# Latent attention: which engine sums the left-over column of the packed values

## The chip, the cores and the metric

The kernel runs on one core of a Trainium2 chip. The metric is the device time of one execution in microseconds (us); lower is better. The engines are called by their names in the profile: PE is TensorE's matmuls, PEld its weight loads, ACT is ScalarE, DVE is VectorE, POOL is GpSimd, SP is SyncE, which here only issues transfers.

## What is computed

The program is one encoder layer over 2048 tokens of width 1024: a Fourier mixing branch, a latent attention with 8 heads, an output projection, a cross attention to 256 memory tokens, and a mixture of 16 experts. The change lies in the latent attention:

```
s = einsum("bqhd,bkhd->bhqk", qn_b, k_nope) + einsum("bqhd,bkd->bhqk", qr_b, k_rope)
p = softmax(s * (64 + 32) ** -0.5)           # over all 2048 keys
o = einsum("bhqk,bkhd->bqhd", p, v)          # 64 channels of v for each head
```

All of it is wanted in float32 precision. The kernel multiplies in a rounded format (fp32r), so it splits operands into a high and a low part and adds the products high by high, high by low and low by high.

## The kernel before

**Work of the attention.** `phase_mla` goes over 32 units, each a head and a block of 512 queries, in an order written out by hand. A unit has 16 key tiles of 128 keys. For a key tile, `scores` makes three matmuls into a PSUM tile `pst` (lines 889 to 891; three such tiles are in turn), then ACT takes the exponential twice: rounded, into the SBUF tile `ph` (line 894), and exact, in place (line 895). DVE subtracts one from the other and gets the low part `pl` (line 909). The values follow three tiles later: `values` multiplies `ph` and `pl` by the value tile and adds into the unit's PSUM tile `po` (line 926).

**The left-over column.** A value tile `va` has 129 columns for each of its 128 keys: 64 columns of the high part, a column of ones that sums the exponentials, 63 columns of the low part, and as column 128 the low part of channel 0, for which the 128 columns of a weight load have no room. Its product with `ph` has to be added to row 0 of `po`. There are two ways. A tile in `BY_PE` gets another matmul with this one column as weights (line 928). For another tile, `ph` is multiplied by the column, a scalar for each partition, and added into an SBUF tile `acc`: POOL multiplies the tiles in `BY_POOL` (line 904), ACT the rest (line 906), both into one of two tiles `part`, and POOL adds (line 908). The first such tile of a unit writes `acc` itself. `whole` then sums `acc` over the partitions with a matmul by ones into row 0 (line 932), in slot 4 of the next unit, and ACT and DVE take the unit's result out of PSUM (lines 935 to 937).

**The order around it.** The loop over slots issues, for each key tile: the scores with their exponentials and the product for the left-over column, a step for the unit after (below), the subtraction, and the values of three tiles before; in 92 of 100 slots a step of the Fourier branch follows, which runs in the background (`bg`) on all engines. The step for the unit after finds the maximum of its scores for each query: 16 matmuls into one of two PSUM tiles `pmax` (line 837), each with a reduction on DVE (line 838). In slot 14 four transposes (line 846) and a copy by ACT (line 847) put the negative maxima into row 96 of the next unit's queries `q`. The third scores matmul of the next unit (line 891) reads that row, so it can't begin before the copy. Each engine executes its own instructions in the order of issue.

Of the kernel before, what the change touches and what calls it, by code (L numbers as in the profile page):

```python
# [10 lines left out]
F = mybir.dt.float32  # L11
R = mybir.dt.float32r
# [3 lines left out]
AF = mybir.ActivationFunctionType  # L16
OP = mybir.AluOpType
# [3 lines left out]
S, D, P = 2048, 1024, 128  # L21
# [9 lines left out]
def pool(ctx, tc, name, bufs=1, **kw):  # L31
    return ctx.enter_context(tc.tile_pool(name=name, bufs=bufs, reuse_waits="tile", **kw))
# [819 lines left out]
def phase_mla(e, keep):  # L852

    nc, tc = e.nc, e.tc
    scale = (ND + RD) ** -0.5
    with ExitStack() as ctx:
# [4 lines left out]
        pp = pool(ctx, tc, "mp", 3, side="right")  # L861
        mp = pool(ctx, tc, "mm", 2, side="right")
# [21 lines left out]
        def scores(h, c, kt):  # L884
            (kh, kl), q = KT[h], QT[h, c]
            qh, ql = q[:, 0], q[0:96, 1]
            p = ps.tile([P, 512], F, name="pst", bufs=3)
            ks = slice(kt * P, (kt + 1) * P)
            nc.tensor.matmul(p, kl[:, ks], qh[0:96], start=True, stop=False)  # L889
            nc.tensor.matmul(p, kh[0:96, ks], ql, start=False, stop=False)  # L890
            nc.tensor.matmul(p, kh[:, ks], qh, start=False, stop=True)  # L891
            ph = pp.tile([P, 512], R, name="ph", bufs=5)
            pl = pp.tile([P, 512], R, name="pl", bufs=3)
            nc.scalar.activation(ph, p, AF.Exp, scale=scale)  # L894
            nc.scalar.activation(p, p, AF.Exp, scale=scale)  # L895

            if kt not in BY_PE:
                w = VT[h, kt // 8][:, kt % 8, 128:129].bitcast(F)
                first = (h, c) not in AC
                if first:  # L900
                    AC[h, c] = mp.tile([P, 512], R, name="acc", bufs=1)
                t = AC[h, c] if first else mp.tile([P, 512], F, name="part", bufs=2)
                if kt in BY_POOL:
                    nc.gpsimd.tensor_scalar(t, ph.bitcast(F), w, None, op0=OP.mult)  # L904
                else:
                    nc.scalar.activation(t, ph.bitcast(F), AF.Copy, scale=w)  # L906
                if not first:
                    nc.gpsimd.tensor_add(AC[h, c], AC[h, c].bitcast(F), t)  # L908
            return ph, pl, lambda: nc.vector.tensor_sub(pl, p, ph.bitcast(F))  # L909

        OT, AC = {}, {}


        BY_PE, BY_POOL = (0, 1, 2, 3, 8, 15), (5, 7, 10, 12)

        rest = mp.tile([64, 1], F, name="rest", bufs=1)
        nc.gpsimd.memset(rest, 1.0)
# [2 lines left out]
        def values(h, c, kt, pr):  # L920

            if kt == 0:
                OT[h, c] = ps.tile([P, 512], F, name="po", bufs=2)
            v = VT[h, kt // 8][:, kt % 8]
            for i, t in enumerate(pr[:2]):
                nc.tensor.matmul(OT[h, c], v[:, 0:128], t, start=kt == 0 and i == 0, stop=False, skip_group_check=True)  # L926
            if kt in BY_PE:
                nc.tensor.matmul(OT[h, c][0:1], v[:, 128:129], pr[0], start=False, stop=False, skip_group_check=True)

        def whole(h, c):  # L930
# [34 lines left out]
        for n, (h, c) in enumerate(units):  # L965
            if n + 3 < len(units):
                load_q(n + 3)
            for kt in range(16):
                if kt in (1, 9) and c == 0 and h + 1 < H:
                    load_k(h + 1, kt // 8)  # L970
                if (c, kt) in ((1, 1), (3, 13)) and h + 1 < H:
                    load_v(h + 1, 4 * c - 4, 4 * c + 4)
                if n and kt == 4:
                    whole(*units[n - 1])
                pend.append((h, c, kt, scores(h, c, kt)))
                for m, i in ahead.get(slot, ()):
                    if i == 0:
                        MX[m] = max_steps(e, QT[units[m]], KT[units[m][0]][0], mp,
                                          lambda shape: ps.tile(shape, F, name="pmax", bufs=2))
                    MX[m][i]()  # L980
                pend[-1][3][2]()
                if len(pend) > 3:
                    values(*pend.pop(0))
                slot += 1
                if slot * RATE // 100 > (slot - 1) * RATE // 100:
                    next(bg, None)
                if (h and c == 0 or n == len(units) - 1) and kt in (4, 8, 12):
                    if kt == 4:
                        rs = recip(e, mp, nc.sync, h - 1) if c == 0 else recip(e, mp, nc.sync, h, 0, 1536)
                    next(rs)  # L990
        for u in pend:
            values(*u)
# [911 lines left out]
def run(e):  # L1904
    e.va_s = e.tc.dram_tile([H, P, 16 * VW], F, name="va_s")
    with ExitStack() as ctx:
        consts(e, ctx)
        pl = pool(ctx, e.tc, "aff")
        e.aff = pl.tile([P, 16, 16], F, name="aff")
        keep = ctx.enter_context(ExitStack())  # L1910
        phase_qkv(e)
        phase_mla(e, keep)
        cross = phase_cross(e)
        phase_out(e, keep, cross)
        for _ in cross:
            pass
        phase_moe(e)
# [141 lines left out]
```

## Time and profile before

| | |
|---|---|
| median of 3 runs | 3174.2 us (3169.05 to 3181.74) |
| the profiled execution's own time | 3177.02 us |
| span of its profile | 3175.2 us |
| mean granted clock of TensorE over the span | 0.972 |
| PE, PEld busy over the span | 2993.6 us (94%), 2583.3 us (81%) |
| DVE, ACT, POOL busy over the span | 1989.3 us (63%), 1669.6 us (53%), 1049.2 us (33%) |

The span is the stretch from the first to the last instruction; some 2 us of the execution lie around it. The attention takes the stretch from 280 to 1298 us. Busy times are unions over an engine's instructions. A matmul's end is modelled, so that the times of matmuls that follow each other overlap: the time that a matmul takes of PE is the distance of its start to the next one's start.

### The profile page before, as it was taken

The page shows a single profiled execution, that of the slowest core. Times are in us where ns is not written, and L with a number is a line of the kernel's source. Part 1 is how long each engine was busy: PE and PEld are TensorE (multiplying, and loading weights), DVE is VectorE, ACT ScalarE, POOL GpSimd, SP SyncE. Part 2 cuts the span into 40 slices and gives each one's busy share as a digit, 9 for nine tenths or more (in the row PEclk, how much of TensorE's full clock was granted, in tenths as well). Part 3 has the DMA queues.
Part 4 walks back from the last instruction along what each step waited for, and adds up shares of the span by engine and source line. Part 5 has one row for each costly group of instructions (what it writes and reads, how often), then busy time and mean ns, then how long its engine had stood idle before and what let it go on. Part 6 is the DMA issues. An engine that isn't in the chain of part 4 may idle for free.

```text
span 3175.2 us, 46609 instructions
## 1 busy us (share of the span) xinstructions
PE 2993.6 (94%) x17759; PEld 2583.3 (81%) x17759; DVE 1989.3 (63%) x3529; ACT 1669.6 (53%) x2715; POOL 1049.2 (33%) x1001
## 2 busy tenths in 40 slices
PE   7998989898999999899999998499999999999998
PEld 6997767677777676689888886499999999999998
DVE  5557877687878787565544445755555555555765
ACT  4445897687778787314433332244444444444554
POOL 1224668768765656200100001200001110002554
PEclk9999999899999999999999999699999999999999
DMA  6666152131121211375211112466666767667885
GB/s 197 208 211 184 41 168 65 28 76 51 44 65 49 68 36 50 100 202 187 90 60 60 61 54 76 135 205 207 199 214 211 216 211 224 204 201 235 298 306 204
DMA packets 314514, 452.51 MB, mean 143 GB/s; under 512 B 21185, under 2 KB 230337, under 8 KB 312946
## 3 DMA queue, kind: packets, MB, share of 16 engines
q1 hardware_dynamic: 282792, 373.08, 36.8%
q0 software_dynamic: 15216, 55.39, 5.7%
q10 hardware_dynamic: 16282, 21.06, 2.3%
q8 instruction: 140, 2.29, 0.3%
q14 instruction: 84, 0.69, 0.1%
HBM read 361.06 MB, written 88.28 MB: 142 GB/s over the span
## 4 chain that ended last, share of the span: by engine, by line
PE 56%; DVE 3%; POOL 1%; ACT 1%; issue 1%; DMA 0%; ACTq 0%; POOLq 0%; DVEq 0%
PE pa L45 5%; PE pa L46 5%; PE pa L47 5%; PE pb L46 5%; PE pb L45 5%; PE pb L47 5%; PE co L45 2%; PE co L47 2%; PE co L46 2%; PE sc L45 2%; PE sc L47 2%; PE sc L46 2%; PE py L45 2%; PE py L47 2%; PE py L46 2%; PE tr L1254 1%
## 5 line engine op out<-in xcount | busy, mean ns | idle before, releaser
L1702 DVE TENSOR_TENSOR wl<-wr,wh 128x2048 fp32r<-128x2048 f32 x188 | 429.6, 2292 | 265.0 <-ACT wh L1701 265.0
L1701 ACT ACTIVATE wh<-wr 128x2048 fp32r<-128x2048 f32 x191 | 362.9, 1908 | 128.9 <-issue 51.5
L909 DVE TENSOR_TENSOR pl<-pst,ph 128x512 fp32r<-128x512 f32 x512 | 351.3, 686 | 120.0 <-ACT pst L895 110.6
L908 POOL TENSOR_TENSOR acc<-acc,part 128x512 fp32r<-128x512 f32 x288 | 376.0, 1306 | 32.1 <-ACT part L906 11.3
L838 DVE TENSOR_REDUCE mt<-pmax 128x1 f32<-128x512 f32 x496 | 338.3, 683 | 68.1 <-PE pmax L837 66.1
L894 ACT ACTIVATE ph<-pst 128x512 fp32r<-128x512 f32 x512 | 304.9, 595 | 135.8 <-PE pst L891 130.5
L895 ACT ACTIVATE pst<-pst 128x512 f32<-128x512 f32 x512 | 305.2, 596 | 0.0
L1737 POOL DMA_INDIRECT x_s<-y,idx x24 | 63.5, 2648 | 730.9 <-ACT y L1872 637.5
L904 POOL TENSOR_SCALAR part<-ph,va 128x512 f32<-128x512 f32 x128 | 205.5, 1606 | 282.4 <-ACT ph L894 158.4
L45 PE MATMUL pa<-hh,wh 128*128 128x256 f32 x1024 | 293.1, 286 | 0.0
L46 PE MATMUL pa<-hl,wh 128*128 128x256 f32 x1024 | 290.7, 284 | 0.1
L47 PE MATMUL pa<-hh,wl 128*128 128x256 f32 x1024 | 290.5, 284 | 0.0
L45 PE MATMUL pb<-hh,wh 128*128 128x256 f32 x1024 | 289.8, 283 | 0.0
L46 PE MATMUL pb<-hl,wh 128*128 128x256 f32 x1024 | 289.8, 283 | 0.0
L47 PE MATMUL pb<-hh,wl 128*128 128x256 f32 x1024 | 289.7, 283 | 0.0
L837 PE MATMUL pmax<-kh,q 96*128 96x512 f32 x496 | 206.4, 418 | 36.6 <-DVE mt L838 18.7
L891 PE MATMUL pst<-q,kh 97*128 97x512 f32 x512 | 208.4, 407 | 26.0 <-ACT q L847 26.0
L889 PE MATMUL pst<-q,kl 96*128 96x512 f32 x512 | 212.1, 414 | 3.2 <-DVE pl L909 2.9
L926 PE MATMUL po<-ph,va 128*128 128x512 f32 x512 | 208.8, 408 | 2.3 <-ACT ph L894 2.3
L926 PE MATMUL po<-pl,va 128*128 128x512 f32 x512 | 207.5, 405 | 1.2 <-DVE pl L909 1.2
L890 PE MATMUL pst<-q,kh 96*128 96x512 f32 x512 | 205.8, 402 | 0.0
L46 PEld LDWEIGHTS pa<-hl,wh 128*128 128x128 f32 x1024 | 197.3, 193 | 1.0 <-DVE hl L38 0.4
(637 smaller groups left out, 7996.1 us busy)
## 6 DMA issues: line engine op xcount, KB each, us to landing
wr<-in_w_exp_gate SPq DMA_DIRECT2D x64, 1024.0 KB
wr<-in_w_exp_up SPq DMA_DIRECT2D x64, 1024.0 KB
wr<-in_w_exp_down SPq DMA_DIRECT2D x63, 1024.0 KB
xr<-in_xT SPq DMA_DIRECT2D x16, 512.0 KB
wr<-in_x SPq DMA_DIRECT2D x16, 512.0 KB
k_s<-put SPq DMA_DIRECT2D x16, 512.0 KB
q<-q_s SPq DMA_DIRECT2D x32, 256.0 KB
wt<-in_xf SPq DMA_DIRECT2D x32, 256.0 KB
```

The source lines that it names most:

```text
L45: nc.tensor.matmul(ps, lh, rh, start=start, stop=False, **kw)
L46: nc.tensor.matmul(ps, lh, rl, start=False, stop=False, **kw)
L47: nc.tensor.matmul(ps, ll, rh, start=False, stop=stop, **kw)
L838: nc.vector.tensor_reduce(mt[:, t, j:j + 1], p, axis=AX.X, op=OP.max)
L889: nc.tensor.matmul(p, kl[:, ks], qh[0:96], start=True, stop=False)
L894: nc.scalar.activation(ph, p, AF.Exp, scale=scale)
L895: nc.scalar.activation(p, p, AF.Exp, scale=scale)
L908: nc.gpsimd.tensor_add(AC[h, c], AC[h, c].bitcast(F), t)
L909: return ph, pl, lambda: nc.vector.tensor_sub(pl, p, ph.bitcast(F))
L926: nc.tensor.matmul(OT[h, c], v[:, 0:128], t, start=kt == 0 and i == 0, stop=False, skip_group_check=True)
L1701: nc.scalar.activation(W[i][0], r, AF.Copy)
L1702: eng.tensor_sub(W[i][1], r, W[i][0].bitcast(F))
```

## The change

The left-over column of ten tiles of a unit (0 to 3, 5, 7, 9, 11, 13, 15) goes to PE and that of six (4, 6, 8, 10, 12, 14) to POOL, which multiplies and adds. Before, six tiles (0 to 3, 8, 15) were PE's, four (5, 7, 10, 12) were multiplied by POOL and six (4, 6, 9, 11, 13, 14) by ACT, and POOL added. The turn of `ph` tiles gets a sixth, the turn of `part` tiles loses its second.

```diff
-            ph = pp.tile([P, 512], R, name="ph", bufs=5)
+            ph = pp.tile([P, 512], R, name="ph", bufs=6)
...
-            if kt not in BY_PE:
+            if kt in BY_POOL:
                 w = VT[h, kt // 8][:, kt % 8, 128:129].bitcast(F)
                 first = (h, c) not in AC
                 if first:
                     AC[h, c] = mp.tile([P, 512], R, name="acc", bufs=1)
-                t = AC[h, c] if first else mp.tile([P, 512], F, name="part", bufs=2)
-                if kt in BY_POOL:
-                    nc.gpsimd.tensor_scalar(t, ph.bitcast(F), w, None, op0=OP.mult)
-                else:
-                    nc.scalar.activation(t, ph.bitcast(F), AF.Copy, scale=w)
+                t = AC[h, c] if first else mp.tile([P, 512], F, name="part", bufs=1)
+                nc.gpsimd.tensor_scalar(t, ph.bitcast(F), w, None, op0=OP.mult)
                 if not first:
                     nc.gpsimd.tensor_add(AC[h, c], AC[h, c].bitcast(F), t)
...
-        BY_PE, BY_POOL = (0, 1, 2, 3, 8, 15), (5, 7, 10, 12)
+        BY_POOL = (4, 6, 8, 10, 12, 14)
...
-            if kt in BY_PE:
+            if kt not in BY_POOL:
                 nc.tensor.matmul(OT[h, c][0:1], v[:, 128:129], pr[0], start=False, stop=False, skip_group_check=True)
```

## Rows read from the trace of the kernel before

**Rows 1.** The page: span; busy time, share and instructions of each engine.

```profile
span 3175.2 us, 46609 instructions
...
PE 2993.6 (94%) x17759; PEld 2583.3 (81%) x17759; DVE 1989.3 (63%) x3529; ACT 1669.6 (53%) x2715; POOL 1049.2 (33%) x1001
```

**Rows 2.** Windows: stretch, length, busy us (instructions) by engine, PEclk, DMA share, GB/s.

```profile
280.00:1298.00 1018.00, 943.49 (x4130) 717.93 (x4129) 775.24 (x1257) 793.96 (x1518) 684.66 (x509) 0.96 0.23 64
...
900.00:1100.00 200.00, 191.52 (x817) 141.78 (x817) 158.06 (x250) 157.35 (x292) 122.27 (x94) 1.00 0.23 62
```

**Rows 3.** Waits of 280 to 1298 us: waiter, releaser; us, times, longest.

```profile
PE pst L891 <- ACT q L847: 26.0, 14, 5.0
PE pmax L837 <- DVE mt L838: 18.7, 20, 2.5
PE pmax L837 <- ACT q L847: 14.4, 3, 6.5
PE pst L889 <- DVE pl L909: 2.9, 5, 1.0
PE pmax L846 <- DVE mt L838: 2.5, 5, 1.0
...
ACT part L906 <- POOL acc L908: 64.0, 45, 6.2
```

**Rows 4.** Timeline of ACT, POOL and PE around the start of unit 26.

```profile
1108.66 0.72 ACT L906 ACTIVATE part<-ph,va 128x512 f32<-128x512 f32 x1 [1.20 <-POOL acc L908]
1109.40 0.59 ACT L847 ACTIVATE q<-pmax 1x512 fp32r<-1x512 f32 x1
...
1107.36 3.95 POOL L908 TENSOR_TENSOR acc<-acc,part 128x512 fp32r<-128x512 f32 x3
...
1107.03 0.40 PE L890 MATMUL pst<-q,kh 96*128 96x512 f32 x1
1110.05 0.50 PE L891 MATMUL pst<-q,kh 97*128 97x512 f32 x1 [2.62 <-ACT q L847]
...
1110.68 0.63 PE L926 MATMUL po<-ph,va 128*128 128x512 f32 x1
1111.10 0.63 PE L926 MATMUL po<-pl,va 128*128 128x512 f32 x1
```

**Rows 5.** Groups by line, 280 to 1300 us: busy us, mean ns, idle before.

```profile
L908 POOL TENSOR_TENSOR acc<-acc,part 128x512 fp32r<-128x512 f32 x288 | 376.0, 1306 | 32.1 <-ACT part L906 11.3
...
L904 POOL TENSOR_SCALAR part<-ph,va 128x512 f32<-128x512 f32 x128 | 205.5, 1606 | 282.4 <-ACT ph L894 158.4 <-PE po L926 89.2 <-PE pst L891 24.6
L906 ACT ACTIVATE part<-ph,va 128x512 f32<-128x512 f32 x160 | 114.7, 717 | 64.3 <-POOL acc L908 64.0
...
L928 PE MATMUL po<-ph,va 128*1 128x512 f32 x192 | 75.9, 395 | 0.0
```

**Rows 6.** Timeline of PE: a matmul of the left-over column and its neighbours.

```profile
1115.59 0.40 PE L926 MATMUL po<-pl,va 128*128 128x512 f32 x1
1115.82 0.39 PE L928 MATMUL po<-ph,va 128*1 128x512 f32 x1
1116.05 0.40 PE L889 MATMUL pst<-q,kl 96*128 96x512 f32 x1
```

**Rows 7.** Timeline of ACT and PE around the start of unit 30.

```profile
1232.96 0.72 ACT L906 ACTIVATE part<-ph,va 128x512 f32<-128x512 f32 x1 [0.38 <-POOL acc L908]
1233.71 0.59 ACT L847 ACTIVATE q<-pmax 1x512 fp32r<-1x512 f32 x1
...
1230.78 0.40 PE L891 MATMUL pst<-q,kh 97*128 97x512 f32 x1
...
1235.53 0.40 PE L891 MATMUL pst<-q,kh 97*128 97x512 f32 x1
```

**Rows 8.** Timeline of POOL: first of six Fourier steps, and the product after the last.

```profile
821.14 2.37 POOL L569 TENSOR_TENSOR d<-x 128x1024 f32<-128x1024 f32 x1
...
833.68 1.56 POOL L904 TENSOR_SCALAR part<-ph,va 128x512 f32<-128x512 f32 x1 [0.20 <-ACT ph L894]
```

## Prediction

> **What bounds the kernel now.** I read the page first, for the span and the busy shares [rows 1], then windows over the attention, since only there are the changed lines at work. The reader is to see two things in them: PE is the busiest engine of that stretch by far, with 943.5 of 1018 us, and its granted clock is 0.96 on average there, while in the stretch from 900 to 1100 us it is 1.00 [rows 2]. So PE sets the time of the attention, and time can be won in two places only: the 74.5 us in which PE is idle, and the 4% of its clock that isn't granted. Whatever is taken from ACT or POOL counts only by these.
>
> Next the waits, to see what ends PE's idle time [rows 3]. 40.4 us in 17 waits (26.0 and 14.4) end with line 847, ACT's copy of the maxima into the queries. Another 24.1 us in 30 waits (18.7, 2.9 and 2.5) end with DVE, mostly its reductions. The last of these rows gives what I take to be behind the first group: ACT itself stands 64.0 us, in 45 waits, at line 906, because both `part` tiles are still with POOL.
>
> The timeline shows how one becomes the other [rows 4]. POOL begins three additions in a row at 1107.36. ACT has to wait 1.20 us before its product of line 906 at 1108.66, and only behind that comes the copy into `q`, at 1109.40. PE has issued line 890 at 1107.03 and can't issue line 891 before 1110.05. It pays a second time after that: its next matmuls stand 0.42 us apart (1110.68 and 1111.10) where 0.23 is the rule [rows 4, 6], so it has fallen to the lower of its two levels, 1.2 GHz, after 2.62 us of idleness.
>
> **Added: matmuls on PE.** Four more tiles of 16 in 32 units are 128 matmuls of line 928. Their mean duration is 395 ns [rows 5], but durations overlap. From the start of one at 1115.82 to the next matmul at 1116.05 is 0.23 us [rows 6], the same as from the matmul before. One column of weights costs as much as 128 then. 128 x 0.23 = 29.4 us, all on the path, because PE has no idle time before line 928 [rows 5] and nothing covers it. The bounds are 0 (all of them fall into idle time that stays) and 128 x 0.395 = 50.6 us. I take 29.4.
>
> The Trainium skill has another figure: its page "TensorE: Matmul & The Clock Gate", section "Back-to-back issue gap", gives some 131 ns for each matmul of 512 columns in a stream of weight loads and matmuls. By an estimate from it the 128 would cost 16.8 us and the forecast would be 12.6 us lower. The trace doesn't agree, with 0.23 us [rows 6].
>
> **Removed: ACT's products.** 192 instructions of 0.717 us [rows 5], 138 us of ACT, and with them the 64.0 us of its waits for POOL. Neither is time of PE. What they give back there has three terms.
>
> *The late copy into `q`.* 40.4 us in 17 waits. A wait costs PE more than the idleness shown, since the shown end of the matmul before it lies 0.16 us behind the next possible start (0.39 against 0.23, [rows 6]): 17 x 0.16 = 2.7, together 43.1 us. Will the copy be in time without the product? At the start of unit 30 [rows 7] it begins at 1233.71, behind a wait of 0.38 and a product of 0.72 us that both go, so it would end near 1233.2 (1233.71 + 0.59 - 1.10), 2.4 us after line 891 of tile 14 was issued at 1230.78. PE reaches line 891 of the next unit at 1235.53; without the six Fourier matmuls in between, some 1.4 us (six times 0.23), it would come there 3.35 us after tile 14. That leaves about 0.9 us, less than two exponentials. I take 39 of 43 us as gone, with 20 as the lower bound (other work of ACT in the way) and 43 as the upper.
>
> *Waits for DVE.* 24.1 us in 30 waits, with 30 x 0.16 = 4.8 some 29 us. DVE's subtraction needs ACT's second exponential, and its reduction for `pmax` stands behind the subtraction; when ACT is stuck, so is DVE. But DVE is also busy for 775 of 1018 us [rows 2], and a part of these waits must be its own. Between 0 and 29 I take 18.
>
> *The clock.* 4% of 1018 us are 41 us of full speed not granted [rows 2]. The stretch from 900 to 1100 us, where PE was busy 96% of the time, shows that it need not be lost. A part of the 41 lies in idle time and costs nothing. If the low stretches go in proportion to the waits removed (57 of the 72 us counted here), that is 32 us, and with a third of it taken off for idle time in them 21. The bounds are 0 and 41.
>
> **Moved at no cost.** POOL's share: 288 additions of 1.306 us become 160, 128 products of 1.606 us become 192 [rows 5], so 581.5 us become 517. What stands in POOL's queue holds up only those who wait for POOL: ACT, for `ph` tiles (a rival below), and PE, for `acc` in slot 4 of the next unit, where it has some six tiles (12 us at 1018 / 512 = 2 us each) for a product and an addition (2.9 us). The one `part` tile is written and read by POOL alone, one after the other. No transfer is issued or moved, and 6 + 1 tiles take the room of 5 + 2. At the very end nothing covers POOL's last product and addition, but they run beside the last tile's exponentials: under 2 us, left out.
>
> **Sum.** 29.4 - 39 - 18 - 21 = -48.6 us, from 3177.0 to 3128.4. The profiled execution is 2.8 us above the median of the runs, so against this the forecast is 3174.2 - 48.6 = 3125.6, say 3125. With each term at its better bound (43, 29, 41, and 0 for the matmuls) the change would be -113, at its worse (20, 0, 0, and 50.6) +31.
>
> **The rivals.**
>
> *A. The added matmuls cost nothing.* They would fill idle time that stays: 3125 - 29 = 3096. For it: PE still has 74.5 us of idleness [rows 2]. Against it: the idleness stands in a few long waits at the unit's ends, while the new matmuls come all over the unit. The Trainium skill, "Perfetto Trace Analysis", section "Identifying the Most-Contended Engine", says that matmul busy time is a poor measure of TensorE's headroom and the share of weight loads a better one. By that rule TensorE, with 718 of 1018 us of weight loads, has some 30% left, and this rival would be the likely one; what the trace shows of it are the equal distances of rows 6, which speak for a full engine. Chance 0.13.
>
> *B. The waits move to DVE.* ACT is free, but DVE, busy 775 of 1018 us, becomes what PE waits for at the unit's ends, where the reductions, the maxima and Fourier work meet. Then 18 becomes 0, a half of the copies stay late (20 for 39) and the clock gives back 8: 29.4 - 20 - 0 - 8 = +1, about 3175. Against it: DVE's subtraction waits for ACT's exponential, and with ACT free its whole queue moves ahead. Chance 0.14.
>
> *C. Slower: GpSimd holds the exponentials.* A `ph` tile is now needed by POOL in six tiles of a unit, and ACT may write it anew six tiles later, 12 us. POOL takes 1.6 + 5 x 2.9 = 16.1 us for a unit's share in tiles 4 to 14, 11 x 2 = 22 us. That fits, but the Fourier branch puts 12.3 us of other steps ahead of a product (821.14 to 833.48, [rows 8]). It decides when POOL falls behind by more than the turn, 12 - 1.6 = 10.4 us; such a burst then costs 2 us, and the four that the branch has cost 8, which the forecast bears. Slower it becomes if POOL is 2.5 us behind the turn in every unit: 32 x 2.5 = 80, so 3205. Chance 0.07.
>
> The forecast holds with 0.66, in its own range from 3103 to 3147.
>
> **Range and chances.** A range of 8 in 10 takes in the forecast's own range, most of rival A and the side of B that wins a little: 3094 to 3156. Outside stay most of B and all of C. A measurement of this kernel tells 0.5%, 16 us, from no change. Faster by more than that (below 3158): 0.66 + 0.13 and 0.03 of B, 0.82. Within it: 0.11. Slower: all of C, 0.07.
>
> **What would show it.** In the profile after: line 906 gone; line 928 with 320 matmuls, still 0.23 us from the next; line 908 with 160 and line 904 with 192 instructions. Waits of PE for line 847 under 6 us in all; those for line 838 about 10. The clock of the attention at 0.98. The attention ends near 1249 us in place of 1298, and what follows is as long as before. The forecast is wrong if PE's idle time stays near 70 us under other names (DVE, or ACT at line 894 waiting for POOL's line 904), if line 891 still waits for line 847, or if the clock stays at 0.96.

## The result, and the profile after

The changed kernel takes 3120.2 us (median of 4 runs, 3117.16 to 3122.51) against 3173.53 us of the kernel before beside it; the ratio is 0.9828 with a 95% interval of 0.9806 to 0.9851. The forecast was 3125 us.

The page of the changed kernel, span and busy time of each engine; its own time was 3118.79 us:

```profile
span 3117.0 us, 46822 instructions
...
PE 2984.5 (96%) x17887; PEld 2580.3 (83%) x17887; DVE 1982.9 (64%) x3529; ACT 1557.5 (50%) x2523; POOL 982.0 (32%) x937
```

Against [rows 1], PE has 128 matmuls more and the span is 58.2 us shorter. The windows show that nearly all of this is the attention, which now ends at 1241 us in place of 1298. The columns are those of [rows 2]:

```profile
280.00:1242.00 962.00, 935.15 (x4257) 715.44 (x4257) 767.72 (x1255) 682.34 (x1326) 616.95 (x445) 0.99 0.24 68
```

Two numbers matter beside [rows 2]. PE is idle for 26.9 us (962.0 - 935.2) in place of 74.5, and its granted clock is 0.99 in place of 0.96. The waits of PE in this stretch answer to [rows 3]:

```profile
PE pmax L837 <- DVE mt L838: 13.2, 9, 8.1
PE po L928 <- POOL acc L905: 4.7, 2, 3.2
PE pmax L837 <- ACT q L847: 2.5, 2, 1.3
...
PE pst L889 <- DVE pl L906: 1.2, 3, 0.5
...
PE pmax L846 <- DVE mt L838: 0.7, 1, 0.7
PE pst L891 <- ACT q L847: 0.2, 1, 0.2
```

The waits for line 847, ACT's copy into `q`, are 2.7 us in 3 waits in place of 40.4 in 17. Those for DVE are 15.1 us in place of 24.1, and 8.1 us of the rest is a single wait, to which the experiments come back. A new name is line 928, the matmul that sums `acc` over the partitions, which waits for POOL.

The groups by line on POOL and PE answer to [rows 5]; ACT has no product any more. The lines there stand one to four lines earlier than before: 903 is POOL's product, 905 its addition, 906 DVE's subtraction, 922 the matmuls of the values, 924 the matmul of the left-over column, 928 the sum over the partitions.

```profile
L903 POOL TENSOR_SCALAR part<-ph,va 128x512 f32<-128x512 f32 x160 | 253.3, 1583 | 98.9 <-ACT ph L894 88.2 <-issue 3.0 <-POOL acc L905 3.0
L905 POOL TENSOR_TENSOR acc<-acc,part 128x512 fp32r<-128x512 f32 x160 | 207.8, 1299 | 13.3
L903 POOL TENSOR_SCALAR acc<-ph,va 128x512 fp32r<-128x512 f32 x32 | 50.5, 1577 | 218.0 <-ACT ph L894 182.4 <-issue 35.6
...
L924 PE MATMUL po<-ph,va 128*1 128x512 f32 x320 | 126.7, 396 | 0.0
```

The longest wait that is left stands in unit 11 (units count from 0). The timeline of ACT, POOL and PE around its start:

```profile
588.73 0.59 ACT L847 ACTIVATE q<-pmax 1x512 fp32r<-1x512 f32 x1
598.31 0.63 ACT L37 ACTIVATE fh<-f 128x512 fp32r<-128x512 f32 x1 [8.99 <-POOL f L585]
...
589.34 2.40 POOL L569 TENSOR_TENSOR d<-x 128x1024 f32<-128x1024 f32 x1
591.82 2.36 POOL L570 TENSOR_TENSOR x<-x 128x1024 f32<-128x1024 f32 x1
594.15 1.56 POOL L903 TENSOR_SCALAR part<-ph,va 128x512 f32<-128x512 f32 x1
595.80 1.26 POOL L905 TENSOR_TENSOR acc<-acc,part 128x512 fp32r<-128x512 f32 x1
597.01 2.51 POOL L585 TENSOR_TENSOR f<-x 128x512 f32<-128x512 f32 x2
...
592.28 0.40 PE L891 MATMUL pst<-q,kh 97*128 97x512 f32 x1
600.73 0.80 PE L837 MATMUL pmax<-kh,q 96*128 96x512 f32 x1 [8.05 <-DVE mt L838]
601.33 0.63 PE L922 MATMUL po<-ph,va 128*128 128x512 f32 x1
601.75 0.63 PE L922 MATMUL po<-pl,va 128*128 128x512 f32 x1
```

ACT's next instruction in order is a step of the Fourier branch, line 37 on `f`, and POOL makes `f` at 597.01 only, behind two long steps and behind a product and an addition for the left-over column. All exponentials stand behind line 37. So DVE, whose name PE's wait bears, waits for ACT, which waits for POOL. After 8.05 us PE starts again at the lower of its two levels, 1.2 GHz: 0.42 us from 601.33 to 601.75, and a granted clock of 0.50 from 600.73 to 604.90. Unit 11 was as long before the change: 40.2 us there and 41.6 here, where a unit is measured from the start of its first score (line 889) to that of the next one's. There the longest wait of line 891 for line 847 in [rows 3], 5.0 us, stood in it, with ACT held for 6.2 us at line 906 while POOL made the same Fourier steps.

### The profile page after: what moved, and what is told of

It is laid out like the page before. It is cut to its first block, busy times and chain, and to the rows that moved or that the text cites. A ratio compares the mean times of both kernels' runs of the same rounds, so it can differ in the third digit from the quotient of the medians.

```text
span 3117.0 us, 46822 instructions
## 1 busy us (share of the span) xinstructions
PE 2984.5 (96%) x17887; PEld 2580.3 (83%) x17887; DVE 1982.9 (64%) x3529; ACT 1557.5 (50%) x2523; POOL 982.0 (32%) x937
## 4 chain that ended last, share of the span: by engine, by line
PE 87%; DVE 4%; ACT 2%; DMA 2%; POOL 2%; issue 1%; SPq 0%; ACTq 0%; POOLq 0%; DVEq 0%
PE po L922 6%; PE pa L45 5%; PE pa L46 5%; PE pa L47 5%; PE pb L45 5%; PE pb L46 5%; PE pb L47 5%; PE pst L889 3%; PE pst L891 3%; PE pmax L837 3%; PE pst L890 3%; PE po L924 2%; PE co L45 2%; PE co L47 2%; PE co L46 2%; PE sc L45 2%
## 5 line engine op out<-in xcount | busy, mean ns | idle before, releaser
L906 DVE TENSOR_TENSOR pl<-pst,ph 128x512 fp32r<-128x512 f32 x512 | 351.7, 687 | 78.9 <-ACT pst L895 74.5
L903 POOL TENSOR_SCALAR part<-ph,va 128x512 f32<-128x512 f32 x160 | 253.3, 1583 | 98.9 <-ACT ph L894 88.2
L905 POOL TENSOR_TENSOR acc<-acc,part 128x512 fp32r<-128x512 f32 x160 | 207.8, 1299 | 13.3
```

## The experiments

Each ran beside the kernel before on the same chip, which took 3174.6 to 3176.5 us there. Where two kernels that ran in different groups are compared, it is by their ratios to it; a difference between two such ratios has a margin of up to 0.003, some 9 us. Lengths of single units come from one profiled execution of each kernel.

**The waiting taken away.** The kernel before with four `part` tiles in place of two, in bfloat16 so that they fit.

```diff
-                t = AC[h, c] if first else mp.tile([P, 512], F, name="part", bufs=2)
+                t = AC[h, c] if first else mp.tile([P, 512], BF, name="part", bufs=4)
```

> The kernel before with four `part` tiles in place of two; to make room they are bfloat16, so the sum of the left-over column is rounded more. ACT still makes its 192 products and PE gets no matmul more. Theory 1 (what PE lost was ACT's waiting for POOL): ACT's waits at line 906 fall from 64 us to under 15, PE's waits for line 847 from 40 us to under 10, the granted clock of the attention rises to 0.98, and the time is 3100 to 3125 us, since no matmul is paid. Rival (what PE lost was the time of the products themselves on ACT): the waits at line 906 go, but those of PE for line 847 stay over 20 us and the time is 3150 us or more.

It took 3123.8 us, ratio 0.9840 (0.9825 to 0.9855). In the groups by line, ACT's product still takes 0.71 us, but the idle time before it is 0.9 us in place of 64.3 [rows 5]:

```profile
L906 ACT ACTIVATE part<-ph,va 128x512 bf16<-128x512 f32 x160 | 114.2, 713 | 0.9 <-POOL acc L908 0.9
```

Among PE's waits, those for line 847 are 5.9 us (3.1 and 2.8):

```profile
PE pmax L837 <- DVE mt L838: 21.1, 17, 9.0
...
PE pmax L837 <- ACT q L847: 3.1, 2, 1.6
PE pst L891 <- ACT q L847: 2.8, 5, 0.7
```

And the window over the attention:

```profile
280.00:1246.00 966.00, 921.85 (x4135) 704.88 (x4134) 772.75 (x1257) 790.98 (x1519) 649.71 (x509) 0.99 0.25 68
```

So 51 us (3174.64 - 3123.8) came from ending ACT's wait for POOL, with no product taken from ACT and no matmul added to PE. The late copy into `q` and the low clock were the effect of that waiting: this is shown here, with ACT busy as before, 791 us, and a clock of 0.99. But the edit does two things at once. It gives ACT room for two more products, and with the narrower type POOL's addition takes 1.185 us in place of 1.306 [rows 5], 35 us less in all:

```profile
L908 POOL TENSOR_TENSOR acc<-acc,part 128x512 fp32r<-128x512 f32 x288 | 341.2, 1185 | 40.9 <-ACT part L906 21.2
```

Which share of the 51 us is due to the room alone, this run doesn't tell.

**ACT's products kept, in the changed order.** The changed kernel, with ACT as the multiplier of its six tiles.

```diff
-                nc.gpsimd.tensor_scalar(t, ph.bitcast(F), w, None, op0=OP.mult)
+                nc.scalar.activation(t, ph.bitcast(F), AF.Copy, scale=w)
...
-            ph = pp.tile([P, 512], R, name="ph", bufs=6)
+            ph = pp.tile([P, 512], R, name="ph", bufs=5)
...
-                t = AC[h, c] if first else mp.tile([P, 512], F, name="part", bufs=1)
+                t = AC[h, c] if first else mp.tile([P, 512], F, name="part", bufs=2)
```

> The changed kernel with the products of its six tiles on ACT in place of POOL (ACT 192 products as before the change, POOL only 160 additions; two `part` and five `ph` tiles as before the change). Theory 1 (ACT's waiting for POOL was the cost, not its products): ACT's waits for POOL at the product under 10 us, PE's waits for line 847 under 8 us, 3112 to 3128 us. Rival (ACT's own time was the cost): PE's waits for line 847 over 20 us and 3145 us or more.

3124.2 us, ratio 0.9844 (0.9829 to 0.9859). With five additions in a unit in place of nine and no products, POOL is never late for ACT's product, and two float32 `part` tiles are enough. In the groups by line of ACT no idle time stands before the product:

```profile
L903 ACT ACTIVATE part<-ph,va 128x512 f32<-128x512 f32 x160 | 114.1, 713 | 0.0
```

And PE's waits for line 847 are 3.7 us at line 837 (and 0.2 at line 891):

```profile
PE pmax L837 <- ACT q L847: 3.7, 2, 1.8
```

Two different ways of ending the wait give 3124 us, and neither takes the 138 us of products from ACT. The rival, that these 50 us were the cost of the products themselves, is out. That both give the same time is chance: this run pays for 128 matmuls more on PE, whose price follows, and the other for four additions and four products more on POOL in each unit of the attention.

The products are not free for all that. Beside the changed kernel, this run differs in who multiplies (and in the two turns of tiles), and its time can't be told from it, 0.9844 beside 0.9828. The lengths of the units show two effects that nearly cancel. Units 11 and 14, where POOL is late through its Fourier steps, take 69.9 us here and 77.3 in the changed kernel. The other thirty take 897.2 us here and 884.6 there, most of it in units 4 and 5, which have much Fourier work on ACT (2.7 us more in each), and in unit 26 (2.1). Two runs below that leave these thirty almost as they are (with five `ph` tiles, and with two light units) give 883.9 and 884.9 us, so the 12.6 us stand out. ACT's products cost PE some 13 us of their own, and POOL's cost 7 in the two units.

**The price of the added matmuls.** The changed kernel without four of the ten matmuls.

```diff
-            if kt not in BY_POOL:
+            if kt in (0, 1, 2, 3, 7, 15):
```

> The changed kernel with the left-over column left out of tiles 5, 9, 11 and 13: 128 matmuls of line 924 fewer, and their part of the result is missing. Theory 1 (each costs PE its 0.23 us): 3120 - 29 = 3091 us, 3085 to 3097. Rival A (they fill idle time): 3115 to 3121 us.

3103.66 us, ratio 0.9776 (0.9761 to 0.9791), so 16.5 us less than the changed kernel: between the two expectations, and both missed. The window over the attention, for the comparison with [rows 2] further below:

```profile
280.00:1222.00 942.00, 908.89 (x4125) 702.38 (x4126) 764.93 (x1253) 680.40 (x1325) 616.69 (x444) 0.99 0.25 69
```

The windows over one unit tell why the price is lower. First unit 18, full of Fourier matmuls, in the changed kernel, without the four, and with all sixteen on PE (the run after this):

```profile
814.10:846.20 32.10, 32.10 (x167) 26.21 (x167) 25.54 (x43) 22.68 (x45) 24.03 (x17) 1.00 0.06 17
```

```profile
805.10:836.20 31.10, 31.10 (x163) 25.89 (x162) 25.39 (x43) 22.65 (x45) 23.85 (x18) 1.00 0.07 17
```

```profile
816.50:849.70 33.20, 33.20 (x172) 26.55 (x170) 25.85 (x43) 22.64 (x44) 3.86 (x3) 1.00 0.06 17
```

PE is busy without a pause in all three, and 163, 167 and 172 matmuls take 31.1, 32.1 and 33.2 us: 0.22 to 0.25 us for each, the 0.23 of [rows 6]. Then unit 5, which has no Fourier matmuls but much Fourier work on ACT, in the changed kernel and without the four:

```profile
416.70:445.00 28.30, 26.25 (x113) 19.32 (x112) 21.01 (x35) 27.19 (x66) 15.86 (x12) 1.00 0.72 227
```

```profile
412.50:442.10 29.60, 25.55 (x108) 18.73 (x107) 21.20 (x35) 27.12 (x66) 15.79 (x12) 1.00 0.71 218
```

Here ACT is busy for 27 us of 28 to 30, PE waits, and four matmuls fewer (five by the windows, whose edges cut at other places) made the unit no shorter. Most units lie between these two. By the lengths of all 32, the four matmuls made a unit 0.6 us or more longer in 21, by 0.2 to 0.6 us in seven, and not longer in units 5, 11, 17 and 21: 18.5 us together. So a matmul costs up to its distance of 0.23 us, by unit, and on average 0.13 us by the times of the runs or 0.14 by these lengths.

**All sixteen tiles on PE.** `BY_POOL` is empty, and line 928 goes.

```diff
-        BY_POOL = (4, 6, 8, 10, 12, 14)
+        BY_POOL = ()
...
-            nc.tensor.matmul(o[0:1], e.ones[:, 0:1], AC.pop((h, c)), start=False, stop=True, skip_group_check=True)
```

> The changed kernel with the left-over column of all sixteen tiles on PE: 192 matmuls of line 924 more, no product or addition on POOL, no sum by ones (32 matmuls fewer). Theory 1 (PE is full, each costs 0.23 us, and POOL's lag goes): 160 x 0.23 = +37, some -13 for the stalls behind POOL, 3144 us, 3138 to 3150. Rival A as far as the run without four tiles bears it out (16.5 us for 128, 0.13 us each, since idle time takes the rest): 160 x 0.13 = +21 - 13, 3128 us, 3122 to 3134.

3126.88 us, ratio 0.9850 (0.9834 to 0.9865): 160 matmuls more cost 7 us on balance, which is not clear of the noise. Theory 1 missed; the time lies in the range of rival A. PE is now busy for 963 of 971 us at a clock of 1.00:

```profile
280.00:1251.00 971.00, 963.42 (x4424) 727.06 (x4423) 768.47 (x1258) 684.13 (x1326) 106.12 (x93) 1.00 0.25 67
```

What POOL's lag had cost pays for most of the matmuls. Unit 11 takes 32.6 us here and 41.6 in the changed kernel; units 11 and 14 together are 12.9 us shorter, and the other thirty, with 150 matmuls more, 20.3 us longer, 0.14 us for each.

**Five `ph` tiles.**

```diff
-            ph = pp.tile([P, 512], R, name="ph", bufs=6)
+            ph = pp.tile([P, 512], R, name="ph", bufs=5)
```

> The changed kernel with five `ph` tiles as before the change in place of six. Theory: POOL's products come late by less than a turn nearly everywhere, so ACT's waits at line 894 for POOL rise from some 6 us to 10 to 25 us, which ACT's idle time mostly covers: 3120 to 3130 us. Rival C in small (POOL holds the exponentials, and the sixth tile is what keeps that from showing): 3140 us or more.

3124.27 us, ratio 0.9841 (0.9826 to 0.9856), which can't be told from the changed kernel. ACT's waits for POOL before line 894 are 17.3 us in place of 5.2:

```profile
ACT ph L894 <- POOL part L903: 12.7, 11, 1.3
...
ACT ph L894 <- POOL acc L905: 4.6, 3, 2.1
```

**Fewer tiles on POOL where it is late.** Units 10 and 13 (the 11th and the 14th) keep tiles 4 and 8 on POOL.

```diff
-        BY_POOL = (4, 6, 8, 10, 12, 14)
+        BY_POOL = lambda h, c: (4, 8) if (h, c) in ((2, 2), (3, 1)) else (4, 6, 8, 10, 12, 14)
```

> The changed kernel, but in two of the 32 units (the 11th and the 14th, where the Fourier branch has long steps on POOL) POOL gets tiles 4 and 8 alone and PE the other fourteen. Theory 1 (the waits left in the next units, 8.1 and 3.2 us on PE with the low clock after them, are POOL's lag): eight matmuls more cost 1.9 us, some 15 us of stalls go, 3107 us, 3103 to 3112. Rival B (they are VectorE's own lateness): the 8 us wait of line 837 for line 838 stays, 3119 to 3124 us.

3108.98 us, ratio 0.9789 (0.9776 to 0.9802). The wait of 8 us is gone; the longest wait of line 837 for DVE is 2.0 us:

```profile
PE pmax L837 <- DVE mt L838: 6.9, 8, 2.0
```

So it was POOL's lag, under DVE's name. Units 11 and 14 became 6.1 and 4.9 us shorter.

**More tiles on POOL where PE is full.** Besides the two light units, eight tiles for POOL in eleven units.

```diff
+        EIGHT = (9, 12, 20, 21, 22, 23, 24, 27, 28, 29, 30)
+        BY_POOL = lambda h, c: (4, 8) if (h, c) in ((2, 2), (3, 1)) else (4, 5, 7, 8, 10, 11, 13, 14) if 4 * h + c in EIGHT else (4, 6, 8, 10, 12, 14)
```

> The kernel with the two light units, 3109 us, and in eleven units that are full of Fourier matmuls but have no long Fourier steps on POOL eight tiles on POOL (4, 5, 7, 8, 10, 11, 13, 14) in place of six: 22 matmuls of line 924 fewer. Theory 1 (PE is full there): 22 x 0.23 = -5, 3104 us, 3101 to 3107. Rival C (POOL with 8 products and 7 additions, some 22 us of 31, falls behind the turn): 3109 us or more.

3111.65 us, ratio 0.9798 (0.9785 to 0.9812): a miss, and no gain. In unit 31, behind the last unit with eight, the sum over the partitions (line 929 here) had to wait 3.7 us for POOL's last addition, and PE's clock fell again. The eleven units are together 3.3 us shorter than in the run with two light units, unit 31 is 4.9 us longer:

```profile
PE po L929 <- POOL acc L905: 5.2, 2, 3.7
```

**The two lessons together.** First, no tile on POOL in the units where that was better; then also eight tiles on POOL in ten units, without the one before the end.

```diff
+        BY_POOL = [() if u in (4, 5, 10, 13, 31) else (4, 6, 8, 10, 12, 14) for u in range(32)]
```

> The changed kernel, but in five of the 32 units (the 5th, 6th, 11th, 14th and 32nd) the left-over column of all sixteen tiles goes to PE; these are the units in which, or in the unit after which, the run with everything on PE was shorter than the changed kernel. Theory 1 (where PE is not full or POOL is behind, matmuls are free; elsewhere they cost 0.23 us): 3109 (two light units) - 4 (what is left of the long wait in the 12th unit) - 3 (5th, 6th, 32nd), 3102 us, 3098 to 3107. Rival (the long wait comes from the Fourier steps on POOL alone, whatever POOL has besides): 3109 us or more.

```diff
+        BY_POOL = [() if u in (4, 5, 10, 13, 31) else (4, 5, 7, 8, 10, 11, 13, 14) if u in (9, 12, 20, 21, 22, 23, 24, 27, 28, 29)
+                   else (4, 6, 8, 10, 12, 14) for u in range(32)]
```

> The same, and eight tiles on POOL in ten units that are full of Fourier matmuls (not in the 31st, after which POOL was late in the run before). Theory 1: twenty matmuls fewer on a full PE, 20 x 0.23 = 4.6, 3098 us, 3094 to 3102. Rival C (POOL falls behind with eight): no shorter than the run without.

The first took 3105.14 us, ratio 0.9775 (0.9762 to 0.9789), with unit 11 at 31.4 us. Its expected time came, but not for every reason given: of the 5th, 6th and 32nd unit only the last became shorter (24.3 us for 25.2), while the others took 29.4 and 29.8 us (27.9 and 28.3 in the changed kernel). The second took 3100.38 us, ratio 0.9762 (0.9748 to 0.9775). It is faster than the changed kernel, since the intervals don't meet, and PE is idle there for 13.7 us of 942, half of the changed kernel's 26.9:

```profile
280.00:1222.00 942.00, 928.35 (x4259) 712.02 (x4259) 766.92 (x1256) 681.77 (x1324) 598.93 (x430) 1.00 0.26 70
```

## Why the prediction was right, step by step

**What bounds the kernel.** Right: PE's idle time and its clock were the two places, and both moved (74.5 to 26.9 us, 0.96 to 0.99), while the 112 us of busy time that left ACT in the attention (794.0 to 682.3) bought little by themselves, some 13 us by the run that keeps the products in the changed order.

**The chain from POOL over ACT to the copy into `q`.** Right, and shown by the run with four `part` tiles: without the wait, 34.5 of the 40.4 us go with the products still on ACT. The run with ACT's products in the changed order, where 3.9 us are left (3.7 and 0.2), says the same without the narrower type.

**The terms of the sum.** The sum came out nearer than its terms: three of them were off, and their errors offset in part. The run without the four matmuls takes them apart, since in the attention its PE has the matmuls of the kernel before (4125 and 4130 in the windows) without the late copies.

The waits were taken at -57 (39 and 18). PE's idle time fell by 41.4 us there (74.5 to 33.1), and its waits from 54 to 26; with 0.16 us for each of these 28, that is some -46. In the changed kernel the waits for line 847 did fall by 37.7 us, as forecast, but those for DVE fell by 9.0 only (8.1 are the lag in unit 11, which stood under line 847 before), and 4.7 us of line 928 are new.

The clock was taken at -21. PE's busy time fell by 34.6 us (943.5 to 908.9); less 4.5 for the modelled ends of those 28 matmuls and 1 for five matmuls fewer, some 29 us are left, and that is an estimate of what the clock gave back. The third taken off for idle time was a guess, and too much.

The matmuls were taken at +29.4, and this term was mis-sized: leaving them out gives back 16.5 us by the times and 18.5 by the units, about halfway to rival A. The distance of 0.23 us holds where PE is full; what failed is that the matmuls are "all on the path" and that "nothing covers it". That PE has no idle time just before line 928 [rows 5] says only that this matmul doesn't wait itself. In a unit in which PE waits later for ACT or DVE, the wait becomes shorter: in unit 5 PE's idle time is 2.05 us with the four matmuls (28.30 - 26.25) and 4.05 without (29.60 - 25.55).

With these figures the sum is -46 - 29 + 18.5 = -56.5, beside -55.6 of the attention in the profiled executions. The forecast of 3125 us lies 5 us from the measured 3120.2 because 11 us too much for the waits and 11 to 13 us too much for the matmuls cancel; what remains is the clock.

The 131 ns that the Trainium skill gives ("TensorE: Matmul & The Clock Gate", "Back-to-back issue gap") would have made it 16.8 us by the estimate, nearly what was measured. The trace doesn't bear out the figure for all that: the distance stays 0.23 us, and the average is low because some of the matmuls fell into idle time.

**The rivals.** A came true by half, in the units where PE isn't full. The rule of the Trainium skill beside it ("Perfetto Trace Analysis", "Identifying the Most-Contended Engine"), that the share of weight loads tells TensorE's headroom, is not borne out: in the run with everything on PE the loads take 727 of 971 us, 75%, and PE has only 7.6 us of idle time left (971.0 - 963.4). B did not come: DVE is the name on the waits that are left, but the run with light units shows POOL behind the longest. C came in small and by another door. ACT was not held by `ph` tiles (5.2 us, and a turn of five changes nothing that can be told), but by a Fourier step that waited for POOL behind a product. With the low clock it cost some 11 us in units 11 and 14 by the run with light units, not every unit as the rival would have needed. Nor was it new: unit 11 took 40.2 us before the change, and units 13 and 14 together 64.8 us before and 62.5 after. It is a gain that the change missed.

**What would show it.** The attention was to end near 1249 us and ended at 1241; the clock was to be 0.98 and is 0.99; waits for line 847 were to be under 6 us and are 2.7; those for line 838 were to be about 10 and are 13.9. What follows the attention was to be as long as before; the span became 2.6 us shorter outside it, 1.1 ahead and 1.5 behind (58.2 - 55.6, with stretches of 1017.9 and 962.3 us from first score to last sum).

What stays open: the run with four `part` tiles (0.9840) is some 20 us longer than the run without products and added matmuls (0.9776), with the same matmuls on PE; 19 us of it lie outside units 11 and 14. About 13 of them fit what ACT's products cost in the changed order. The rest may be POOL's larger share there (busy 649.7 us against 616.7), and no run separates that.

## What to carry to other kernels

An engine that has no work to spare can be lost to an engine two steps away: look for instructions that wait, in an in-order queue, ahead of the one that the busiest engine needs, and first try to end that wait by more buffers. Here two more, in a narrower type that also made POOL's additions shorter, won 51 us, as much as the whole change with its 53. The price of work added to the busiest engine is its issue distance only in the stretches where that engine has no pause, so price it stretch by stretch. Where the background load differs by unit, a fixed split among engines is too coarse: choosing it by unit, from the traces, won another 20 us.

## What was not expected of the hardware

The busiest engine can take more work and get almost nothing longer: 160 matmuls more on PE cost 7 us, because PE no longer waited for POOL (7.6 us of idle time in place of 26.9) and its granted clock was 1.00 in place of 0.99. Idle times of 2.62 us [rows 4] and 8.05 us were both followed by matmuls 0.42 us apart, so a wait of PE costs more than its own length.
